# A two-block transformer kernel: the first weight tiles behind a juncture are split by VectorE, later ones wait for the last sums, and the lead's second loads come later

## The chip, the cores and the metric

One NeuronCore of a Trainium2 chip. The metric is the device time of one execution, in microseconds. The engines are called PE (TensorE, matrix products), DVE (VectorE), ACT (ScalarE), POOL (GpSimd) and SP (SyncE, which here only issues DMAs); each works through its own instructions in a fixed order, and semaphores hold an instruction back until what it needs is done.

## The reference

Two depth-2 stacks run one after the other on 512 tokens of width 1024, in fp32: two attention layers (here "block1"), then two layers of FFN, token mixer, FFN. Each branch is normed, projected, and its output is normed again and added to x.

```python
def rms_norm_2(x, gain):
    xf = x.astype(jnp.float32)
    y = xf * lax.rsqrt(jnp.mean(xf * xf, axis=-1, keepdims=True) + NORM_EPS)
    return (y * gain).astype(x.dtype)

def swiglu(h, w_in, w_out):
    gu = h @ w_in
    g, u = jnp.split(gu, 2, axis=-1)
    return (jax.nn.silu(g) * u) @ w_out
...
def second_block(x, norm_gain, ffn_w_in, ffn_w_out, mix_w_in, ...):
    for layer in range(DEPTH):
        g = norm_gain[layer]
        h = swiglu(rms_norm_2(x, g[0]), ffn_w_in[layer, 0], ffn_w_out[layer, 0])
        x = x + 0.5 * rms_norm_2(h, g[1])
        h = token_mixer(rms_norm_2(x, g[2]), mix_w_in[layer], ...)
        x = x + rms_norm_2(h, g[3])
        h = swiglu(rms_norm_2(x, g[4]), ffn_w_in[layer, 1], ffn_w_out[layer, 1])
        x = x + 0.5 * rms_norm_2(h, g[5])
    return x
```

The first stack (`first_block`) is two layers of `x + rms_norm(attention(rms_norm(x) @ w_in) @ w_out)`. The branches in order are block1, block1, ffn0, mixer0, ffn1, ffn2, mixer1, ffn3.

## The kernel before

**Products.** Every fp32 operand is kept as a high and a low part, and each product is three matmuls (`mm3`, L353 high by high, L354 and L355 high by low). x is held transposed, `XT`, as 8 chunks of 128 features by 512 tokens; its high and low parts are `xh` and `xl`.

**Weights.** A weight comes in raws of 128x1024 fp32 (512 KB, tile `wr`, two buffers), loaded by SP (L395). `wsplit` takes a raw in two tiles of 128x512: ACT writes the high part `wh` (L419), then POOL, or DVE where `lo` says so, subtracts it from the raw and writes the low part `wl` (L421). `wh` and `wl` have six buffers each. So a raw's buffer comes free when its second `wl` is written, and PE can use a weight chunk's high part before the low part is there.

**Juncture.** Between two branches stands a `Join`: for both halves of the tokens (t = 0, 1) and four pairs of chunks (i), `front` scales the branch's output and adds it to XT on DVE (L281 or, where a gain of 0.5 is applied, L285; then L287), ACT writes `xh` (L289) and squares (L495), POOL adds the squares up (`sacc`, L498 and L501), and `back` writes `xl` on DVE (L299). `third` does this for t = 1. While this runs, PE already works on the next branch's first two weight units, its "lead" (`lead`): first for t = 0, then for t = 1, one pair of chunks after another as their `xh` and `xl` appear. The row norm itself is applied behind the products, from the sums: a chain of nine small DVE operations (L364 to L372), a transpose that spreads its result (tile `tp`, L438) and an ACT copy (tile `R`, L536). The lead's own weights are loaded and split ahead of the juncture, by `lead_load`, with DVE splits (`lo=nc.vector`, pinned).

**Order.** The kernel is written in program order and a scheduler sets each engine's order when it is built. Two tools bind it: `tc.keep_in_program_order` pins an instruction among the others that are pinned, and `tc.issue_after(x)` holds an instruction behind `x`. `k.gate` uses the second for POOL's weight splits behind a juncture: set at (t, i) == (0, 3), it lets the next eight of them issue only behind the last sum of the first half.

**FFN.** Behind the lead (hidden tiles j = 0 and 1) an FFN takes hidden tiles j = 2, 3, ... over all 512 tokens: per tile two raws (h = 0, 1), 8 chunks, two PSUM banks and 48 matmuls. j = 2 writes to `mm` banks, later ones to `sc`. `act` is on DVE and ACT: `fg` = gate * R (L607), silu (L608), `fu` = up * R (L609), product (L610), high part `ah` on ACT (L611) and low part `al` on DVE (L612). For the lead `act` runs per half: once R of t = 0 is there, and again when R of t = 1 is there. Then four `out_unit`s (p = 0 to 3) multiply by ffn_out, DVE adds the halves (L633). In p = 2 of the second half, `lead_load` loads and splits both parts of the next branch's lead.

The mixer and block1 have the same lead; in block1 the first unit behind it is `tok(0)` (its weights are the stationary operand, 128x256 products), where DVE rotates the results (`ra`, `rb`, L963). In the last unit of `out_proj` (mixer, block1) `lead_load` is called as in the FFN.

Of the kernel before, what the change touches and what calls it, by code (L numbers as in the profile page):

```python
# [210 lines left out]
class Join:  # L211
# [52 lines left out]
    def third(self):  # L264
        self.spread(1)
        self.front(1, 0)
        for i in range(1, 4):
            self.front(1, i)
            self.back(1, i - 1)
        self.back(1, 3)  # L270

    def front(self, t, i):

        k, nc, put = self.k, self.nc, self.put
        v = nc.vector
        sl, c = HALF[t], slice(2 * i, 2 * i + 2)
        if t not in self.scratch:
            self.scratch[t] = (k.mm if t else k.sc)().rearrange("p (a n) -> p a n", a=2)
        s, P = self.scratch[t], self.P[t]
        if self.gpost is None:  # L280
            put(v.tensor_tensor(s, self.Y[:, c, sl], P[:, None, :].to_broadcast([128, 2, 256]), op=OP.mult))  # L281
        else:
            for e in range(2):
                j = 2 * i + e
                put(v.scalar_tensor_tensor(s[:, e], self.Y[:, j, sl], self.gpost[:, j:j + 1], P, op0=OP.mult, op1=OP.mult))  # L285
        x = k.XT[:, c, sl]
        put(v.tensor_tensor(x, x, s, op=OP.add))  # L287
        for j in (2 * i, 2 * i + 1):
            nc.scalar.activation(k.h[0][:, j, sl], k.XT[:, j, sl], AF.Copy, scale=k.gcol(self.nxt[0], j))  # L289
        added = k.square2(k.pre[t], i, x)  # L290
        if (t, i) == (0, 3):
            k.gate = [added, 8]
# [20 lines left out]
class Kern:  # L313
    def __init__(self, ctx, tc, ap):
# [14 lines left out]
        self.gate = None  # L329

# [67 lines left out]
    @contextmanager  # L398
    def behind(self, eng):


        if self.gate and eng is self.nc.gpsimd:
            self.gate[1] -= 1
            with self.tc.issue_after(self.gate[0]):
                yield
            if not self.gate[1]:
                self.gate = None
        else:
            yield

    def wsplit(self, raw, n, lo=None, pool=None, pin=False):
        nc = self.nc
        w = []
        eng = lo or nc.gpsimd
        for c in range(0, n, 2):
# [4 lines left out]
            with self.behind(eng):  # L420
                ins = eng.tensor_tensor(low[:, :m], raw[:, c:c + m], hi[:, :m].bitcast(F32), op=OP.subtract)  # L421
            if pin:
                self.tc.keep_in_program_order(ins)
# [128 lines left out]
    def lead_load(self, nxt, lo=None):  # L552

        if nxt:
            self.lead_w = [[], []]
            for h in range(2):
                for u in range(2):
                    self.lead_w[u] += self.wload(nxt[1][u][h], lo=lo, pool=self.lead_pool, pin=True)
# [35 lines left out]
    def ffn(self, i, gpost, nxt):  # L594
# [19 lines left out]
        def out_unit(half, p):  # L614
            w = []
            for c0 in range(0, FH, 4):
                n = min(4, FH - c0)
                w += self.wload(ap["ffn_out"][i, half, p, :, c0:c0 + n], n)
            last = half == 1 and p == 3
            if half == 1 and p == 2:  # L620
                self.lead_load(nxt, lo=nc.vector)
            for sl in HALF if last else [slice(0, S)]:
                for b in range(2):
                    ps = self.mm()[:, 0:sl.stop - sl.start]
                    for k in range(FH):
                        self.mm3(ps, self.wcol(w[k], slice(b * 128, (b + 1) * 128)), [x[:, sl] for x in acts[k]],
                                 k == 0, k == FH - 1)
                    k = p * 2 + b
# [130 lines left out]
    def out_proj(self, w_ap, OT, gpost, nxt):  # L759
# [7 lines left out]
        with ExitStack() as es:  # L767
            own = Pool(es.enter_context(self.tc.tile_pool(name=f"op{self.leads}", bufs=1, reuse_waits="tile")))
            jobs = [(0, ALL), (1, ALL)] + [(p, h) for h in HALF for p in (2, 3)]
            for p, sl in jobs:  # L770
# [4 lines left out]
                if p == 2 and sl.start == 0:  # L775
                    self.lead_load(nxt, lo=nc.vector)
# [191 lines left out]
    def block1_lead(self, l):  # L968
        return G_PRE + l, (self.ap["w_in"][l, 8], self.ap["w_in"][l, 11])
# [217 lines left out]
    def mixer_lead(self, l):  # L1187
        return G_NORM + l * 6 + 2, (self.ap["mix_in"][l, 6], self.ap["mix_in"][l, 7])

    def ffn_lead(self, l, i):  # L1190
        return G_NORM + l * 6 + 4 * i, (self.ap["ffn_in"][2 * l + i, 0], self.ap["ffn_in"][2 * l + i, 1])
# [308 lines left out]
    def run(self, nl1, nl2):  # L1500
# [15 lines left out]
        self.lead_load(branches[0][2], lo=self.nc.vector)  # L1516
# [96 lines left out]
```

## Time and profile before

| | |
|---|---|
| time, median of 3 runs (lowest to highest) | 2846.74 us (2845.9 to 2852.84) |
| profiled execution: its time, its span | 2845.98 us, 2844.0 us |
| PE busy, share of the span | 2741.8 us, 96% |
| DVE, ACT, POOL busy | 1412.6, 1374.1, 1356.5 us |
| `wl` on POOL (L421) | 732 instructions, mean 1297 ns, 942.0 us |
| `wl` on DVE (L421) | 104 instructions, mean 889 ns |
| PE waited for `xl` (L299) | 16.2 us, 21 times, at most 1.3 us |
| mean granted PE clock | 0.992 of full |

The span is that of the profiled execution; its own time lies 2.0 us over it. In a row of the timeline the first number is the start from the span's begin, the second the duration, both in us; `xcount` is how many like instructions a row stands for (its time is then that from the first's start to the last's end), and the bracket gives the engine's idle time before the row and what ended it. The starts of PE's rows are what to go by: a matmul's shown duration overlaps the next one's.

### The profile page before, as it was taken

Reading aid. Unit: us, or ns where it says so; the run is one execution under the profiler, and the core shown is the slowest. Engines: PE = TensorE matmul, PEld = TensorE weight load, DVE = VectorE, ACT = ScalarE, POOL = GpSimd, SP = SyncE. Lnnn points to the kernel's source line nnn. Section 1 sums busy time; section 2 is a strip of 40 time slices with the busy share of each in tenths; the row PEclk is TensorE's granted clock in tenths of the full one; section 3 lists DMA queues with packets and bytes.
Section 4 is the critical chain, followed back from the end, with each engine's and each line's share of the span. In section 5 each row is a group of like instructions: output and inputs, shape, how many; then the busy total and the mean of one; then the engine's idle time right before and its main releaser. Section 6 shows DMA issues by size and latency. Waiting matters only on the chain.

```text
span 2844.0 us, 42873 instructions
## 1 busy us (share of the span) xinstructions
PE 2741.8 (96%) x16080; PEld 2398.0 (84%) x16080; DVE 1412.6 (50%) x2988; ACT 1374.1 (48%) x2881; POOL 1356.5 (48%) x1327
## 2 busy tenths in 40 slices
PE   8999999999999999899999999999998899999998
PEld 8997899788888887898988888888887798888887
DVE  6589757986302266747630225312336747731132
ACT  5678547874333335657433334333334758433332
POOL 4553365424444455443544445444455543544545
PEclk9999999999999999999999999999999999999999
DMA  5111221112333222121223232233222120223332
GB/s 176 60 46 38 75 72 46 45 66 75 96 92 103 85 81 83 51 79 62 78 96 96 97 93 93 89 89 104 95 77 86 62 81 31 90 82 91 105 99 77
DMA packets 69280, 230.53 MB, mean 81 GB/s; under 512 B 8968, under 2 KB 11912, under 8 KB 68816
## 3 DMA queue, kind: packets, MB, share of 16 engines
q1 hardware_dynamic: 69072, 227.78, 24.5%
q8 instruction: 127, 2.08, 0.3%
q14 instruction: 81, 0.66, 0.1%
HBM read 225.51 MB, written 2.24 MB: 80 GB/s over the span
## 4 chain that ended last, share of the span: by engine, by line
PE 74%; DVE 15%; ACT 4%; issue 3%; POOL 2%; DMA 2%; SPq 0%; POOLq 0%; DVEq 0%; ACTq 0%
PE sc L354 11%; PE sc L353 11%; PE sc L355 11%; PE mm L355 11%; PE mm L353 11%; PE mm L354 11%; DVE xl L299 2%; PE sc L116 2%; PE tp L145 1%; DVE pl L149 1%; DVE XT L287 1%; DVE nm L192 1%; DVE E L204 1%; PE tp L817 1%; POOL wl L421 1%
## 5 line engine op out<-in xcount | busy, mean ns | idle before, releaser
L421 POOL TENSOR_TENSOR wl<-wr,wh 128x512 fp32r<-128x512 f32 x732 | 942.0, 1297 | 883.0 <-ACT wh L419 858.9
L419 ACT CAST wh<-wr 128x512 fp32r<-128x512 f32 x836 | 500.5, 612 | 722.8 <-PE sc L354 450.9
L354 PE MATMUL sc<-xl,wh 128*128 128x512 f32 (+1 forms) x1824 | 658.0, 361 | 16.3 <-DVE xl L299 16.2
L355 PE MATMUL sc<-xh,wl 128*128 128x512 f32 (+1 forms) x1824 | 654.5, 359 | 0.2 <-DVE wl L421 0.2
L353 PE MATMUL sc<-xh,wh 128*128 128x512 f32 (+1 forms) x1824 | 653.2, 360 | 0.0
L607 DVE TENSOR_TENSOR fg<-sc,R 128x512 f32<-128x512 f32 (+1 forms) x92 | 59.3, 644 | 747.6 <-PE sc L355 724.5
L354 PEld LDWEIGHTS sc<-xl,wh 128*128 128x128 f32 x1824 | 344.0, 189 | 72.1 <-DVE xl L299 20.7
L355 PEld LDWEIGHTS sc<-xh,wl 128*128 128x128 f32 x1824 | 344.2, 189 | 51.8 <-DVE wl L421 0.4
L353 PEld LDWEIGHTS sc<-xh,wh 128*128 128x128 f32 x1824 | 342.5, 189 | 51.5
L355 PE MATMUL mm<-ah,wl 128*128 128x512 f32 (+1 forms) x792 | 291.0, 367 | 6.5 <-POOL wl L421 6.5
L353 PE MATMUL mm<-ah,wh 128*128 128x512 f32 (+1 forms) x792 | 290.3, 367 | 1.9 <-ACT wh L419 1.9
L354 PE MATMUL mm<-al,wh 128*128 128x512 f32 (+1 forms) x792 | 289.3, 365 | 0.0
L353 PE MATMUL mm<-wh,xh 128*128 128x256 f32 x960 | 275.0, 286 | 0.0
L354 PE MATMUL mm<-wl,xh 128*128 128x256 f32 x960 | 273.2, 285 | 0.0
L355 PE MATMUL mm<-wh,xl 128*128 128x256 f32 x960 | 273.0, 284 | 0.0
L353 PE MATMUL mm<-xh,wh 128*128 128x512 f32 (+1 forms) x560 | 196.7, 353 | 10.5 <-DVE big L789 3.4
L355 PE MATMUL mm<-xh,wl 128*128 128x512 f32 (+1 forms) x560 | 194.8, 348 | 7.8 <-POOL wl L421 7.8
L354 PE MATMUL mm<-xl,wh 128*128 128x512 f32 (+1 forms) x560 | 193.9, 346 | 0.0
L354 PEld LDWEIGHTS mm<-wl,xh 128*128 128x128 f32 x960 | 184.1, 192 | 1.3
L353 PEld LDWEIGHTS mm<-wh,xh 128*128 128x128 f32 x960 | 183.9, 192 | 1.0
L355 PEld LDWEIGHTS mm<-wh,xl 128*128 128x128 f32 x960 | 184.0, 192 | 0.9
L355 PEld LDWEIGHTS mm<-ah,wl 128*128 128x128 f32 x792 | 149.2, 188 | 33.8 <-POOL wl L421 9.6
(348 smaller groups left out, 4878.1 us busy)
## 6 DMA issues: line engine op xcount, KB each, us to landing
wr<-in_ffn_in_dram SPq DMA_DIRECT2D x176, 512.0 KB, 3.3
wr<-in_ffn_out_dram SPq DMA_DIRECT2D x64, 512.0 KB, 3.6
wr<-in_mix_in_dram SPq DMA_DIRECT2D x56, 512.0 KB, 3.3
wr<-in_w_in_dram SPq DMA_DIRECT2D x48, 512.0 KB, 3.3
wr<-in_ffn_out_dram SPq DMA_DIRECT2D x32, 384.0 KB, 3.1
wr<-in_w_out_dram SPq DMA_DIRECT2D x16, 512.0 KB, 3.3
wr<-in_mix_out_dram SPq DMA_DIRECT2D x16, 512.0 KB, 3.3
Mb<-Md SPq DMA_DIRECT2D x16, 256.0 KB, 3.1
```

The source lines that it names most:

```text
L116: nc.tensor.matmul(sc[:, e], q, kk[:, :n], start=j == 0, stop=j == len(self.K) - 1)
L145: nc.tensor.transpose(p[:, j * per + e], E[i + e][:, j * 128:(j + 1) * 128], self.k.ident)
L149: nc.vector.tensor_tensor(pl[:, :nk, sl], pv, ph[:, :nk, sl].bitcast(F32), op=OP.subtract)
L192: nc.vector.tensor_reduce(nm, sc, axis=AX.X, op=OP.max, negate=True)
L204: nc.vector.scalar_tensor_tensor(E[tb, 0], E[tb, 1], cc[:, i:i + 1], E[tb, 0], op0=OP.mult, op1=OP.add)
L299: self.put(self.nc.vector.scalar_tensor_tensor(lo, k.XT[:, j, sl], k.gcol(self.nxt[0], j), hi.bitcast(F32), op0=OP.mult, op1=OP.subtract))
L353: mm(out, lhs[0], rhs[0], start=start, stop=False, skip_group_check=shared)
L354: mm(out, lhs[0], rhs[1], start=False, stop=False, skip_group_check=shared)
L355: mm(out, lhs[1], rhs[0], start=False, stop=stop, skip_group_check=shared)
L419: nc.scalar.copy(hi[:, :m], raw[:, c:c + m])
L421: ins = eng.tensor_tensor(low[:, :m], raw[:, c:c + m], hi[:, :m].bitcast(F32), op=OP.subtract)
L607: nc.vector.tensor_tensor(g, ps[0], R[:, sl], op=OP.mult)
```

## The change

Three parts:

1. At the start of `third`, `k.ahead` is set to 6 (3 where the next branch is a mixer). The next `ahead` weight tiles that POOL would split go to DVE, pinned in program order. There are seven junctures with a next branch: five with 6 and two with 3, so 36 splits move.
2. The gate is set at (t, i) == (1, 3), for the 8 - `ahead` splits that follow on POOL: these wait for the last sum of the second half.
3. `lead_load` takes h: the lead's first raws come at p = 2, its second ones at p = 3. In the FFN, `out_load(p + 1)` stands at the end of unit p, ahead of its last DVE addition, where the load and its splits stood at the start of unit p + 1.

```diff
     def third(self):
         self.spread(1)
+        self.k.ahead = self.nxt[2]
         self.front(1, 0)
...
-        if (t, i) == (0, 3):
-            k.gate = [added, 8]
+        if (t, i) == (1, 3):
+            k.gate = [added, 8 - k.ahead]
...
-    @contextmanager
-    def behind(self, eng):
-        if self.gate and eng is self.nc.gpsimd:
-            self.gate[1] -= 1
-            with self.tc.issue_after(self.gate[0]):
-                yield
...
     def wsplit(self, raw, n, lo=None, pool=None, pin=False):
...
-        eng = lo or nc.gpsimd
...
             nc.scalar.copy(hi[:, :m], raw[:, c:c + m])
-            with self.behind(eng):
+            eng, held, order = lo or nc.gpsimd, None, pin
+            if eng is nc.gpsimd and self.ahead:
+                self.ahead -= 1
+                eng, order = nc.vector, True
+            elif eng is nc.gpsimd and self.gate:
+                self.gate[1] -= 1
+                held = self.gate[0]
+                if not self.gate[1]:
+                    self.gate = None
+            with self.tc.issue_after(held) if held else nullcontext():
                 ins = eng.tensor_tensor(low[:, :m], raw[:, c:c + m], hi[:, :m].bitcast(F32), op=OP.subtract)
-            if pin:
+            if order:
                 self.tc.keep_in_program_order(ins)
...
-    def lead_load(self, nxt, lo=None):
+    def lead_load(self, nxt, h, lo=None):
         if nxt:
-            self.lead_w = [[], []]
-            for h in range(2):
-                for u in range(2):
-                    self.lead_w[u] += self.wload(nxt[1][u][h], lo=lo, pool=self.lead_pool, pin=True)
+            if h == 0:
+                self.lead_w = [[], []]
+            for u in range(2):
+                self.lead_w[u] += self.wload(nxt[1][u][h], lo=lo, pool=self.lead_pool, pin=True)
...
         def out_unit(half, p):
-            w = []
+            if not ahead:
+                out_load(half, p)
+            w = ahead[:]
+            ahead.clear()
             last = half == 1 and p == 3
-            if half == 1 and p == 2:
-                self.lead_load(nxt, lo=nc.vector)
+            if half == 1 and p >= 2:
+                self.lead_load(nxt, p - 2, lo=nc.vector)
...
+                    if b and p < 3:
+                        out_load(half, p + 1)
```

The built programs show where the scheduler put the moved splits. In each row below, the first number is the place on its engine, then come line, operation and tiles (numbers behind a name tell buffers and raws apart), and what the instruction waits for. DVE, at the start of ffn1's work behind its lead: before, the last `al` of the first half is followed by the second half's rms chain.

```order
1831 L612 TENSOR_TENSOR al_16504<-fu_16506,ah_16503 128x256 [waits Activation_49]
1832 L612 TENSOR_TENSOR al_16514<-fu_16516,ah_16513 128x256 [waits Activation_49]
1833 L364 TENSOR_SCALAR rnx_16557<-tp_16554 128x2 [waits PE_49]
...
1851 L612 TENSOR_TENSOR al_16514<-fu_16621,ah_16513 128x256 [waits Activation_49]
1852 L610 TENSOR_TENSOR fu_16637<-fu_16637,fg_16636 128x512 [waits DVE_49]
1853 L612 TENSOR_TENSOR al_16635<-fu_16637,ah_16634 128x512 [waits Activation_49]
1854 L607 TENSOR_TENSOR fg_16716<-sc_16644,R_16118 128x512 [waits PE_49]
```

The same place on DVE of the changed kernel:

```order
1846 L611 TENSOR_TENSOR al_16504<-fu_16506,ah_16503 128x256 [waits Activation_49]
1847 L611 TENSOR_TENSOR al_16514<-fu_16516,ah_16513 128x256 [waits Activation_49]
1848 L420 TENSOR_TENSOR wl_16535<-wr_16532,wh_16534 128x512 [waits DMAHW5_49]
1849 L420 TENSOR_TENSOR wl_16539<-wr_16532,wh_16538 128x512
1850 L366 TENSOR_SCALAR rnx_16557<-tp_16554 128x2 [waits PE_49]
...
1871 L609 TENSOR_TENSOR fu_16637<-fu_16637,fg_16636 128x512 [waits DVE_49]
1872 L611 TENSOR_TENSOR al_16635<-fu_16637,ah_16634 128x512 [waits Activation_49]
1873 L420 TENSOR_TENSOR wl_16649<-wr_16646,wh_16648 128x512 [waits DMAHW1_49]
1874 L420 TENSOR_TENSOR wl_16653<-wr_16646,wh_16652 128x512
1875 L606 TENSOR_TENSOR fg_16716<-sc_16644,R_16118 128x512 [waits PE_49]
```

The splits of j = 2 (`wl_16535`, `wl_16539`) now stand behind the last `al` of the first half, and those of j = 3 (`wl_16649`, `wl_16653`) behind j = 2's own `al_16635`. On POOL of before, these four stand at rows 662, 663, 669 and 670, between the sums of the two halves.

PE of before, where j = 2 starts (`mm_16530`, `mm_16531`):

```order
8055 L353 MATMUL mm_16530<-xh_84,wh_16534 128x512 [waits PE_49]
8056 L354 MATMUL mm_16530<-xl_85,wh_16534 128x512
8057 L355 MATMUL mm_16530<-xh_84,wl_16535 128x512 [waits Pool_49]
8058 L353 MATMUL mm_16531<-xh_84,wh_16534 128x512
8059 L354 MATMUL mm_16531<-xl_85,wh_16534 128x512
```

PE of the changed kernel, at the start of j = 2 and of j = 3 (`sc_16644`, `sc_16645`):

```order
8055 L355 MATMUL mm_16530<-xh_84,wh_16534 128x512 [waits PE_49]
8056 L356 MATMUL mm_16530<-xl_85,wh_16534 128x512
8057 L355 MATMUL mm_16531<-xh_84,wh_16534 128x512
8058 L356 MATMUL mm_16531<-xl_85,wh_16534 128x512
8059 L472 MATMUL tp_16554<-ones_94,sacc_16308 128x1 [waits PE_49,Pool_49]
8060 L472 MATMUL tp_16554<-ones_94,sacc_16308 128x1
8061 L357 MATMUL mm_16530<-xh_84,wl_16535 128x512 [waits DVE_49]
...
8107 L355 MATMUL sc_16644<-xh_84,wh_16648 128x512 [waits Activation_49]
8108 L356 MATMUL sc_16644<-xl_85,wh_16648 128x512
8109 L355 MATMUL sc_16645<-xh_84,wh_16648 128x512
8110 L356 MATMUL sc_16645<-xl_85,wh_16648 128x512
8111 L357 MATMUL sc_16644<-xh_84,wl_16649 128x512 [waits DVE_49]
```

The four products that need only the high part are pulled together ahead of the first that needs the low part, and that one waits for DVE now. Third place, ACT of before in the last `out_unit`s of ffn0, where `wr_11619` and `wr_11629` are the lead's second raws and `wr_11721` is ffn_out's first raw of p = 3:

```order
1053 L419 CAST wh_11631<-wr_11629 128x512 [waits DMAHW7_49]
1054 L419 CAST wh_11635<-wr_11629 128x512
1055 L485 ACTIVATE sq_11674<-big_9312 128x256 [waits DVE_49,Pool_49]
1056 L485 ACTIVATE sq_11677<-big_9312 128x256 [waits Pool_49]
1057 L419 CAST wh_11723<-wr_11721 128x512 [waits DMAHW4_49,PE_49]
```

The same rows of the changed kernel, where the lead's second raws are called `wr_11731` and `wr_11741` and ffn_out's is `wr_11694`:

```order
1053 L407 CAST wh_11743<-wr_11741 128x512 [waits DMAHW7_49]
1054 L407 CAST wh_11747<-wr_11741 128x512
1055 L484 ACTIVATE sq_11654<-big_9312 128x256 [waits DVE_49,Pool_49]
1056 L484 ACTIVATE sq_11657<-big_9312 128x256 [waits Pool_49]
1057 L407 CAST wh_11696<-wr_11694 128x512 [waits DMAHW4_49,PE_49]
```

The names have changed, and the places by content have not: the lead's casts stand ahead of those of p = 3 in both.

## Rows read from the trace of the kernel before

**Rows 1.** The page: the span, and each engine's busy time.

```profile
span 2844.0 us, 42873 instructions
...
PE 2741.8 (96%) x16080; PEld 2398.0 (84%) x16080; DVE 1412.6 (50%) x2988; ACT 1374.1 (48%) x2881; POOL 1356.5 (48%) x1327
```

**Rows 2.** Timeline of the juncture ahead of ffn1, second half: POOL, DVE, PE.

```profile
1388.89 2.70 POOL L421 TENSOR_TENSOR wl<-wr,wh 128x512 fp32r<-128x512 f32 x2
...
1389.22 2.65 DVE L299 SCALAR_TENSOR_TENSOR xl<-XT,gains,xh 128x256 fp32r<-128x256 f32 x2
...
1390.50 0.38 PE L354 MATMUL sc<-xl,wh 128*128 128x256 f32 x1 [1.21 <-DVE xl L299]
...
1397.22 0.39 PE L354 MATMUL sc<-xl,wh 128*128 128x256 f32 x1 [0.43 <-DVE xl L299]
```

**Rows 3.** Line L299 by itself: durations ns, smallest, median, largest.

```profile
L299 DVE SCALAR_TENSOR_TENSOR xl<-XT,gains,xh x112: 467/950/1510, 346.0 to 2486.2; 128x256 fp32r<-128x256 f32 x112
```

**Rows 4.** Timeline of the juncture ahead of mixer0, second half: PE.

```profile
1048.87 0.39 PE L354 MATMUL sc<-xl,wh 128*128 128x256 f32 x1 [1.34 <-DVE xl L299]
...
1052.80 0.39 PE L354 MATMUL sc<-xl,wh 128*128 128x256 f32 x1 [0.81 <-DVE xl L299]
```

**Rows 5.** Timeline of ffn1 behind its lead: PE's j = 2, DVE's and ACT's `act`.

```profile
1403.16 0.40 PE L353 MATMUL mm<-xh,wh 128*128 128x512 f32 x1
...
1404.79 0.76 DVE L610 TENSOR_TENSOR fu<-fu,fg 128x256 f32<-128x256 f32 x2 [0.31 <-ACT fg L608]
...
1405.25 0.41 ACT L611 CAST ah<-fu 128x256 fp32r<-128x256 f32 x1 [0.18 <-DVE fu L610]
...
1405.68 0.43 DVE L612 TENSOR_TENSOR al<-fu,ah 128x256 fp32r<-128x256 f32 x1
...
1405.90 0.50 PE L473 MATMUL tp<-ones,sacc 128*128 128x1 f32 x4
...
1406.26 0.49 PE L353 MATMUL mm<-xh,wh 128*128 128x512 f32 x1
```

**Rows 6.** Timeline of DVE in ffn0's last units: two splits back to back.

```profile
1007.52 1.29 DVE L421 TENSOR_TENSOR wl<-wr,wh 128x512 fp32r<-128x512 f32 x2 [5.04 <-ACT wh L419]
```

**Rows 7.** Timeline of ffn1: the second half's `act`, and PE's start of j = 3.

```profile
1414.03 0.42 DVE L607 TENSOR_TENSOR fg<-sc,R 128x256 f32<-128x256 f32 x1 [4.25 <-ACT R L536]
...
1414.80 0.39 PE L353 MATMUL sc<-xh,wh 128*128 128x512 f32 x1
...
1419.63 1.01 DVE L612 TENSOR_TENSOR al<-fu,ah 128x512 fp32r<-128x512 f32 x1 [0.69 <-ACT ah L611]
```

**Rows 8.** Windows (start:end length; engines' busy us; PEclk third from the end).

```profile
1170.00:1172.30 2.30, 0.01 (x1) 0.01 (x1) 0.75 (x2) 1.75 (x6) 2.16 (x3) 1.00 0.00 0
...
1173.10:1179.60 6.50, 6.29 (x25) 5.74 (x25) 5.44 (x19) 2.31 (x10) 2.66 (x4) 0.50 0.35 121
...
1110.77:1114.90 4.13, 4.13 (x10) 3.27 (x11) 0.00 (x0) 0.00 (x0) 3.66 (x3) 0.50 0.39 126
...
1762.30:1766.00 3.70, 3.08 (x23) 2.82 (x23) 3.63 (x5) 2.29 (x6) 3.54 (x5) 1.00 0.65 237
```

**Rows 9.** Waits of PE by releaser: us in total, times, longest us.

```profile
PE mm L355 <- POOL wl L421: 14.4, 17, 3.9
```

**Rows 10.** Timeline of the second block1 behind its lead: PE's first product, DVE.

```profile
377.62 0.28 PE L353 MATMUL mm<-wh,xh 128*128 128x256 f32 x1
...
380.25 0.14 DVE L1015 TENSOR_SCALAR subg<-subg 128x1 f32<-128x1 f32 x1
...
390.04 0.42 DVE L963 TENSOR_TENSOR ra<-mm,lin 128x256 f32<-128x256 f32 x1 [3.50 <-POOL wl L421]
```

**Rows 11.** Timeline of mixer0 behind its lead: DVE, PE's first product.

```profile
1062.20 1.29 DVE L1201 TENSOR_TENSOR O<-sc,R 128x512 f32<-128x512 f32 x2 [1.74 <-ACT R L536]
...
1062.30 0.40 PE L353 MATMUL mm<-xh,wh 128*128 128x512 f32 x1
```

**Rows 12.** Timeline of ACT in ffn0's last units: the lead's second raw.

```profile
1006.87 1.14 ACT L419 CAST wh<-wr 128x512 fp32r<-128x512 f32 x2 [6.59 <-DMA wr<-in_mix_in_dram]
```

More of the change, by code (lines that the diff above doesn't have):

```diff
@@ L1 @@
 import math
-from contextlib import ExitStack, contextmanager
+from contextlib import ExitStack, nullcontext
 import numpy as np
@@ L329, in __init__ @@
         self.gate = None
+        self.ahead = 0
     def tp(self):
@@ L396, in wload @@
         return self.wsplit(raw, n, lo, pool, pin)
-    @contextmanager
-    def behind(self, eng):
-        if self.gate and eng is self.nc.gpsimd:
-            self.gate[1] -= 1
-            with self.tc.issue_after(self.gate[0]):
-                yield
[L406 to L409, printed above, removed]
     def wsplit(self, raw, n, lo=None, pool=None, pin=False):
@@ L612, in act, with out_load, out_unit @@
             nc.vector.tensor_tensor(al, u, ah.bitcast(F32), op=OP.subtract)
-        def out_unit(half, p):
-            w = []
+        ahead = []
+        def out_load(half, p):
             for c0 in range(0, FH, 4):
                 n = min(4, FH - c0)
-                w += self.wload(ap["ffn_out"][i, half, p, :, c0:c0 + n], n)
+                ahead.extend(self.wload(ap["ffn_out"][i, half, p, :, c0:c0 + n], n))
+        def out_unit(half, p):
+            if not ahead:
+                out_load(half, p)
+            w = ahead[:]
+            ahead.clear()
             last = half == 1 and p == 3
-            if half == 1 and p == 2:
-                self.lead_load(nxt, lo=nc.vector)
+            if half == 1 and p >= 2:
+                self.lead_load(nxt, p - 2, lo=nc.vector)
             for sl in HALF if last else [slice(0, S)]:
@@ L774, in out_proj @@
                     ws[p] += self.wload(w_ap[p][1], pool=pool, raws=self.wp)
-                if p == 2 and sl.start == 0:
-                    self.lead_load(nxt, lo=nc.vector)
+                if p >= 2 and sl.start == 0:
+                    self.lead_load(nxt, p - 2, lo=nc.vector)
                 for b in range(2):
@@ L968, in block1_lead @@
     def block1_lead(self, l):
-        return G_PRE + l, (self.ap["w_in"][l, 8], self.ap["w_in"][l, 11])
+        return G_PRE + l, (self.ap["w_in"][l, 8], self.ap["w_in"][l, 11]), 6
     def block1(self, l, nxt):
@@ L1187, in mixer_lead @@
     def mixer_lead(self, l):
-        return G_NORM + l * 6 + 2, (self.ap["mix_in"][l, 6], self.ap["mix_in"][l, 7])
+        return G_NORM + l * 6 + 2, (self.ap["mix_in"][l, 6], self.ap["mix_in"][l, 7]), 3
     def ffn_lead(self, l, i):
-        return G_NORM + l * 6 + 4 * i, (self.ap["ffn_in"][2 * l + i, 0], self.ap["ffn_in"][2 * l + i, 1])
+        return G_NORM + l * 6 + 4 * i, (self.ap["ffn_in"][2 * l + i, 0], self.ap["ffn_in"][2 * l + i, 1]), 6
     def mixer(self, l, nxt):
@@ L1515, in run @@
             self.load_x()
-        self.lead_load(branches[0][2], lo=self.nc.vector)
+        for h in range(2):
+            self.lead_load(branches[0][2], h, lo=self.nc.vector)
         self.prenorm(branches[0][2][0])
```

## The prediction

> **What bounds the kernel now.** I read the page first. PE is busy 2741.8 us of a span of 2844.0 [rows 1], so about 102 us of its idle time is all there is to win, and whatever makes PE wait is lost at once. I then went through PE's waits in the timeline and looked at what stands ahead of each. At the junctures it is `xl`. With POOL's splits running beside it (1388.89, 2.70 us for two), two `xl` take 2.65 us, and PE waits 1.21 and later 0.43 us [rows 2]. Alone an `xl` takes as little as 0.467 us [rows 3], so each takes 1.3 where it could take half a microsecond. At the junctures with the 0.5 gain PE waits 1.34 and 0.81 us [rows 4]. That is the stall the change goes at. Then I read the stretch just behind the juncture, where PE does not wait at all today: that is where the moved splits now stand, so I took every duration there.
>
> **What the removal of POOL's splits from the second half gives.** With no split beside it, the first `xl` of 1389.22 ends at about 1389.69 in place of 1390.44, so the wait of 1.21 shrinks to 0.47; the wait of 0.43 goes. That is 1.17 us per juncture [rows 2, 3]. There are four of this form (ahead of the second block1, ffn0, ffn1, ffn3). At the other three (ahead of mixer0, ffn2, mixer1) the first wait falls by 0.82 (the first `xl` there took 1.30) and the second by its 0.81, so 1.63 [rows 3, 4]. Together 4 x 1.17 + 3 x 1.63 = 9.6 us. From below: nothing, if POOL's running sums, which stay, slow `xl` by themselves (its median is 0.950 [rows 3]).
>
> **What the moved splits cost at an FFN's start.** DVE works in order. The splits of j = 2 now stand behind the first half's `act`, those of j = 3 behind j = 2's. Before, both were done on POOL before PE came there.
>
> First wait. PE starts j = 2 at 1403.16; 12 products until 1405.90 give 0.23 us each [rows 5]. In the changed order it can do four products (0.91) and the ones-products (1406.26 less 1405.90, 0.36) and wants the first low part at 1404.43. DVE ends the second `fu` at 1405.55, ACT the second `ah` 0.41 after the first, at 1406.07, and `al` takes 0.43, so the split starts at 1406.50 [rows 5]. A split takes 0.65 on DVE where POOL is quiet [rows 6], and the low part is there at about 1407.2. **PE waits 2.8 us.**
>
> Second wait. Counted from the second half's R, which moves along with PE: DVE starts its `act` at 1414.03 and j = 2's own `al` at 1419.63, PE starts j = 3 at 1414.80 [rows 7]. PE wants j = 3's low part four products later, at 1415.7. That `al` took 1.01 beside a POOL split; alone I take 0.7 (the split of the same size, rows 6), so the split starts at 1420.3 and ends at 1421.0. **PE waits 5.3 us** (5.6 with 1.01). The raws behind these two splits come free later too, but the next ones are wanted a full hidden tile (48 products, 11 us) later; a load, a cast and a POOL split have to fit in that, and I count nothing there. All four FFNs start with this order.
>
> **What the waits do to PE's clock.** After PE had been idle from 1170.00 to 1172.30, its granted clock was 0.50, the 1.2 GHz level, from 1173.10 for 6.5 us; after the wait that ended at 1110.77 it was 0.50 until 1114.90, 4.13 us [rows 8]. That wait is the longest one for a POOL split, 3.9 us [rows 9]. After the wait of 1.33 that ended at 1762.30 it stayed 1.00 [rows 8]. At half clock half of the time is lost. For the first wait (2.8) the nearest row is the one of 2.30: at most 3.2 us lost, and less if the low level begins within the wait, so 2.6. For the second (5.3) the nearest is that of 3.9: 2.1. Both lie between 0 (no fall) and 3.2.
>
> The Trainium skill (TensorE: Matmul & The Clock Gate, HAM oscillation — how this bites in real kernels) says that PE drops to its lower clock after long idle gaps between bursts and pays for each again, and the trace agrees for the gap of 3.9. By that rule gaps below its limit cost nothing, the first wait might be one of them, and the sum would be some 13 us lower; the fall after 2.30 us speaks against it. This is one of the rivals below, worked out there from rows.
>
> So an FFN's start costs 2.8 + 5.3 + 2.6 + 2.1 = 12.8, four of them 51.2, and with their gains (3 x 1.17 + 1.63 = 5.1) **+46.1 us**.
>
> **The second block1.** Its four first splits stand on DVE behind `subg`, which ends at 380.39; PE, from 377.62, wants the first at 378.2 (two products at half of 0.23, as they are half as wide, and the ones-products), and has it at 381.1 [rows 6, 10]. Wait 2.9, clock 2.6. The next two splits stand behind the four rotations of the unit's second half, about 1.4 to 1.7 (0.42 each, overlapping), and PE wants them at once: 1.4 + 0.7 - 0.2 = 1.9 [rows 6, 10]. A wait of 1.9 lies between the 1.33 that left the clock alone and the 2.30 that did not; I take no fall. Less 1.17: **+6.2**.
>
> **The mixers.** Only three splits move. They stand behind two `O` (to 1063.49); the low part is there at 1064.15 and wanted at 1062.30 + 0.92 + 0.36 = 1063.6, a wait of 0.55 [rows 5, 6, 11]. The third split stands inside the second rms chain and may hold PE as long again, up to 0.85; I take 1.0 for both. No clock. Less 1.63: **-0.6 each, -1.3** for two.
>
> **The lead's second loads.** In the last `out_unit`s ACT waits 6.59 us for the lead's second raw, and the casts of p = 3 stand behind it [rows 12]. The code moves the call, but the built order of ACT and SP is the same by content as before, so this wait stays: 0. DVE's splits of that raw now stand behind the additions of p = 2 and run beside POOL's splits of p = 3; that may add up to 0.4 per FFN, and nothing waits for the splits themselves before the juncture. At `out_proj` the order is unchanged as well.
>
> **Sum.** 46.1 + 6.2 - 1.3 = +51.0. On the profiled execution's 2845.98 that is 2897.0. The median of the three runs is 2846.74, 0.8 above it, which I leave aside: **2897 us**.
>
> **The rivals.**
> - *The first, shorter waits leave the clock alone*: without 4 x 2.6 and block1's 2.6 the sum is 51.0 - 13.0 = 38.0, 2884 us. For it: no row shows a gap of just 2.8. Against it: 2.30 was enough at 1172.30 [rows 8]. This is the case of the Trainium skill's rule named above.
> - *No fall at all*: another 4 x 2.1 less, +29.6, 2876 us. Against it: the row of 1110.77 [rows 8].
> - *The sums slow `xl` as the splits did*, and the gain of 9.6 is not there: +60.6, 2907 us. For it: the median of 0.950 [rows 3]. Against it: PE waits longest just where a split lies beside `xl` [rows 2].
> - *The later loads do free p = 3*: the casts there stop waiting [rows 12], and I bound the gain by 3 us in each of three FFNs: 2888 us. Against it: the built order.
> - *The other side: DVE has time.* If the moved splits are done before PE wants them, only the gains are left: 2845.98 - 9.6 = 2836 us. The place is DVE between 1403 and 1406.5: this decides as soon as the two waits of an FFN's start together fall below 1.2 us, in place of 8.1. The pieces of `act` ahead of the splits would have to take almost no time [rows 5, 7].
> - *A draw*: waits so short, with no clock, that they cancel the gains, 2846 us.
>
> **How the numbers follow.** Forecast 0.52, first waits without clock 0.18, no clock 0.08, no gain at `xl` 0.09, p = 3 freed 0.05, DVE in time 0.05, a draw 0.03. This kernel's time can be told from no change at about 0.3%, 8.5 us. Faster by more: 0.05; within: 0.03; slower: 0.92. The bounds: with no clock 2876, less 2 for the reading of the durations, is 2874; with 3.2 us for each of the FFNs' eight waits and for both of block1's (the second had none) in place of what I took, 4 x (0.6 + 1.1) + 0.6 + 3.2 = 10.6 more, 2908, and 3 for the longer `al` (0.3 x 4) and the splits of p = 3 gives 2911. The range 2874 to 2911 leaves out the two cases at 2836 and 2846 and the tails.
>
> **What would show it.** In the changed profile: PE waits for DVE's `wl` (L420) of 2 to 3 us at each FFN's start and of about 5 us at its j = 3, some 40 us in all; a granted clock of 0.50 behind them; `xl` below its mean of before, and the waits for it down from 1.2 to 0.5; the ACT wait of 6.6 us ahead of p = 3 unchanged. If PE's waits for DVE's `wl` are short, the prediction is wrong at its first step, and if they are long and the clock stays at 1.00, at its third.

## The result, and the profile after

The changed kernel takes 2890.61 us (median of four; 2886.42 to 2894.36) and the kernel before 2848.49 (four runs): ratio 1.0146, interval 1.0133 to 1.0158. It is slower by 42 us by the medians. The two profiled executions, 2894.36 (the slowest of its four) and 2845.98 us, lie 48.4 apart, and it is this difference that the rows below explain. The prediction was 2897, its range 2874 to 2911. All ratios are of fast executions alone, while the medians 2850.38 and 2852.18 below include one slow execution each (3811 and 3017 us).

The page of the changed kernel, against [rows 1]: the span grew by 47.9 us, PE's busy time by 15.7 of them.

```profile
span 2891.9 us, 42851 instructions
...
PE 2757.5 (95%) x16080; PEld 2409.4 (83%) x16080; DVE 1421.9 (49%) x3024; ACT 1373.8 (48%) x2881; POOL 1306.5 (45%) x1291
```

PE's waits by releaser (us in total, times, longest). Two lines are new, 29.6 us for splits on DVE, nearly all of it at the FFNs' starts (the second block1's 2.6 us stand in a third). The waits for `xl`, 16.2 us before, are down to 6.5.

```profile
PE sc L357 <- DVE wl L420: 19.2, 5, 4.7
...
PE mm L357 <- DVE wl L420: 10.4, 6, 2.5
...
PE sc L356 <- DVE xl L300: 6.5, 11, 0.9
```

The timeline of the changed kernel where ffn1 starts, PE, DVE and ACT in order of time, answers to [rows 5] and [rows 7]. PE does four products of j = 2 and the ones-products and then waits. DVE has the first half's `act` ahead of the two splits: its `fu` waits for the silu of ACT, which itself waits for R (1420.64) and loads a table for 1.28 us; `al` and the splits follow without a gap, and the first split ends just before PE goes on. At j = 3 the same happens behind j = 2's own `act`.

```profile
1420.64 0.37 ACT L535 COPY R<-tp 128x256 f32<-128x256 f32 x1 [4.14 <-PE tp L437]
1421.03 1.28 ACT L607 ACT_TABLE_LOAD   x1
1421.15 0.40 PE L355 MATMUL mm<-xh,wh 128*128 128x512 f32 x1
...
1422.77 0.76 DVE L609 TENSOR_TENSOR fu<-fu,fg 128x256 f32<-128x256 f32 x2 [0.31 <-ACT fg L607]
1423.67 0.76 DVE L611 TENSOR_TENSOR al<-fu,ah 128x256 fp32r<-128x256 f32 x2
1424.35 1.29 DVE L420 TENSOR_TENSOR wl<-wr,wh 128x512 fp32r<-128x512 f32 x2
1425.09 0.73 PE L357 MATMUL mm<-xh,wl 128*128 128x512 f32 x2 [2.51 <-DVE wl L420]
...
1435.42 0.39 PE L355 MATMUL sc<-xh,wh 128*128 128x512 f32 x1
...
1439.89 0.69 DVE L611 TENSOR_TENSOR al<-fu,ah 128x512 fp32r<-128x512 f32 x1 [0.69 <-ACT ah L610]
1440.50 1.28 DVE L420 TENSOR_TENSOR wl<-wr,wh 128x512 fp32r<-128x512 f32 x2
1441.24 1.22 PE L357 MATMUL sc<-xh,wl 128*128 128x512 f32 x2 [4.75 <-DVE wl L420]
```

Windows of the changed kernel just behind such waits (PEclk is the third figure from the end): ffn1's first wait, ffn1's second, ffn3's first, ffn0's first, ffn0's second, ffn2's first. Only the first window, behind a wait of 2.51 us, has the full clock. Behind the other waits PE ran at the 1.2 GHz level, also where the wait was as long (ffn3, 2.51) or shorter (ffn2, 2.31).

```profile
1425.20:1428.50 3.30, 3.30 (x15) 2.73 (x16) 3.01 (x12) 0.00 (x0) 0.00 (x0) 1.00 0.49 159
1441.30:1446.80 5.50, 5.50 (x13) 4.33 (x14) 0.48 (x1) 1.47 (x3) 1.06 (x1) 0.50 0.52 194
...
2533.00:2536.00 3.00, 3.00 (x8) 2.31 (x8) 1.71 (x6) 0.79 (x2) 0.00 (x0) 0.50 0.64 190
...
697.10:700.50 3.40, 3.40 (x8) 2.75 (x9) 3.05 (x12) 0.00 (x0) 0.00 (x0) 0.50 0.49 154
...
716.10:720.00 3.90, 3.90 (x9) 3.05 (x10) 0.46 (x1) 0.06 (x1) 0.00 (x0) 0.50 0.61 209
...
1805.80:1808.80 3.00, 3.00 (x8) 2.35 (x9) 2.72 (x12) 0.00 (x0) 0.00 (x0) 0.50 0.53 176
```

**Where the 48 us went.** I compared the start of the same PE product in both traces. At ffn1, j = 2 starts at 1403.16 before and at 1421.15 after, 17.99 later; j = 3 at 1414.80 and 1435.42, 20.62 later. So the first wait cost 2.6. By the middle of j = 3 (1422.96 and 1451.43) the lag is 28.5: the second cost 7.9. Over the four FFNs:

| | ffn0 | ffn1 | ffn2 | ffn3 | sum | PE's idle time in it |
|---|---|---|---|---|---|---|
| first wait | 5.5 | 2.6 | 4.0 | 4.3 | 16.4 | 9.8 |
| second wait | 7.0 | 7.9 | 7.9 | 6.7 | 29.4 | 19.0 |

So the FFN starts cost 45.8 us, of which 28.8 are idle time; 17.0 are not. The second block1 lost 7.9 us behind its lead, and ffn0's p = 3 lost 2.8. At the seven junctures PE came 13.0 us earlier in all (1.5 to 2.3 each); the mixers and smaller places lost 4.4 of that again.

### The profile page after: what moved, and what is told of

Read it like the earlier page. It is cut to its first block, busy times and chain, and to the rows that moved or that the text cites. A ratio compares the mean times of both kernels' runs of the same rounds, so it can differ in the third digit from the quotient of the medians.

```text
span 2891.9 us, 42851 instructions
## 1 busy us (share of the span) xinstructions
PE 2757.5 (95%) x16080; PEld 2409.4 (83%) x16080; DVE 1421.9 (49%) x3024; ACT 1373.8 (48%) x2881; POOL 1306.5 (45%) x1291
## 4 chain that ended last, share of the span: by engine, by line
PE 73%; DVE 15%; ACT 5%; issue 3%; POOL 2%; DMA 1%; SPq 0%; POOLq 0%; DVEq 0%; ACTq 0%
PE sc L357 11%; PE sc L356 11%; PE sc L355 11%; PE mm L357 11%; PE mm L355 10%; PE mm L356 10%; PE sc L116 2%; PE tp L145 1%; DVE pl L149 1%; POOL wl L420 1%; DVE xl L300 1%; DVE nm L192 1%; DVE wl L420 1%; DVE E L204 1%; PE tp L825 1%
## 5 line engine op out<-in xcount | busy, mean ns | idle before, releaser
L420 POOL TENSOR_TENSOR wl<-wr,wh 128x512 fp32r<-128x512 f32 (+1 forms) x696 | 893.4, 1293 | 935.1 <-ACT wh L407 888.0
L357 PE MATMUL mm<-ah,wl 128*128 128x512 f32 (+1 forms) x792 | 291.8, 368 | 10.4 <-POOL wl L420 10.3
L357 PE MATMUL mm<-xh,wl 128*128 128x512 f32 (+1 forms) x560 | 197.2, 354 | 18.2 <-DVE wl L420 10.4
```

The costliest lines, as they stand in the source:

```text
L357: mm(out, lhs[1], rhs[0], start=False, stop=stop, skip_group_check=shared)
```

## The experiments

**Each part alone.** First the gate alone: in the kernel before, `(t, i) == (0, 3)` becomes `(1, 3)`, and all eight splits stay on POOL.

> The kernel before with the gate's place alone changed: set at (1, 3) with a count of 8, all splits stay on POOL. If the loss comes from where the splits stand on DVE, nothing of it is here: the waits for xl fall from 16.2 to about 6.5 us as in the changed kernel, POOL starts j = 2's splits behind the last sum and has the first done before PE wants it, no wait for a wl of more than 0.5 us at an FFN's start, and the time is 10 to 13 us under before (ratio 0.9955 to 0.9965). If holding POOL's splits back is itself what costs (late low parts, raws freed late), the waits for wl show here on POOL and the time is 10 us or more above before.

Measured: 2863.15 us against 2850.55, ratio 1.0043 (1.0030 to 1.0056). Neither theory had this. The waits for `xl` did fall, and no low part was late, but a new wait took their place:

```profile
PE tp L438 <- DVE r L372: 17.7, 7, 2.9
...
PE sc L354 <- DVE xl L299: 6.4, 11, 0.9
```

Its timeline at the juncture ahead of ffn1 (POOL, DVE, PE) shows why. POOL starts its four splits as soon as the last sum is done, just when DVE runs the first half's rms chain. The chain's operations on 128x2 take 0.16 us when POOL is quiet; here four in a row take 1.2 each, and each ends within 0.1 us of a POOL split's end.

```profile
1405.23 4.99 POOL L421 TENSOR_TENSOR wl<-wr,wh 128x512 fp32r<-128x512 f32 x4
1405.33 1.21 DVE L366 TENSOR_TENSOR rnt<-r 128x2 f32<-128x2 f32 x1
1406.57 1.22 DVE L367 SCALAR_TENSOR_TENSOR rnt<-rnt,rnx 128x2 f32<-128x2 f32 x1
1407.82 1.20 DVE L368 SCALAR_TENSOR_TENSOR r<-rnt,r 128x2 f32<-128x2 f32 x1
1409.05 1.18 DVE L369 TENSOR_TENSOR rnt<-r 128x2 f32<-128x2 f32 x1
1410.27 0.16 DVE L370 TENSOR_TENSOR rnt<-rnt,rnx 128x2 f32<-128x2 f32 x1
...
1410.97 0.41 PE L438 MATMUL tp<-ident,r 128*128 128x128 f32 x2 [2.54 <-DVE r L372]
```

So the later hold moves the collision from `xl` to the chain. In the changed kernel at ffn1 POOL has no split to run there, since the moved ones are on DVE, and PE has no wait for the chain's `r` at any juncture.

Then the moved splits alone, with the gate set at (0, 3) and the loads as before, and the third part alone (gate and splits as before).

> The first part alone: 36 splits go to DVE, pinned; the gate is set at (0, 3) as before (with 8 less the splits moved), and the lead's loads come as before. If DVE's order is the cause, the waits of 2.5 and 4.7 us at each FFN's start are all here, and the time is 43 to 48 us above before (ratio 1.015 to 1.017), a little less than the whole change by what p = 3 costs there. If the gate or the loads carry a good part of the loss, it is under +30 us.

> The third part alone: the lead's second raws at p = 3 and out_load at the unit's end; no split moves and the gate is as before. By the built order the casts stand where they stood, so the wait of ACT of 6.6 us stays; DVE's four splits of these raws run beside POOL's of p = 3 and each slows the other (1.72 in place of 1.28 us on POOL in the changed kernel), so 0 to 4 us above before (ratio 1.000 to 1.0015). If the later loads freed p = 3, it is 5 to 9 us under before; if they are a main part of the loss, 10 us or more above.

Measured: 2888.97 us, ratio 1.0134 (1.0120 to 1.0147), 38 us above the kernel before (43 to 48 expected), with the same two waits (19.0 and 10.4 us) and the same 6.5 us for `xl`; and 2850.38 us, ratio 0.9994 (0.9985 to 1.0004). So the loss is that of the moved splits, and the gain at `xl` is theirs too. The gate's later place costs something by itself (above), but beside the moved splits nothing of it can be measured: 1.0134 without it and without the later loads, 1.0146 with both, and the intervals overlap. The third part does nothing that can be measured either.

**Four splits in place of six** at block1 and the FFNs:

```diff
-        return G_NORM + l * 6 + 4 * i, (...), 6
+        return G_NORM + l * 6 + 4 * i, (...), 4
```

> The whole change with 4 in place of 6 splits moved (mixers still 3): the splits of j = 3 stay on POOL, behind the last sums. If each wait has its own price, the second waits (4.7 us, and the 1.2 GHz stretch behind each) are gone and the first stay: 4 x (4.7 + 1.9) + 1.6 for the second block1, so 28 us under the changed kernel, some 17 to 20 above before (ratio 1.006 to 1.007). If the second wait only takes over what the first leaves (the same lateness passed on), the time is within 10 us of the changed kernel.

Measured: 2858.48 us, ratio 1.0028 (1.0017 to 1.0039), 32 us under the changed kernel (28 expected). PE's second waits are gone, since j = 3's splits are on POOL again; the first stay, as the waits of this run show:

```profile
PE mm L357 <- DVE wl L420: 10.4, 6, 2.5
```

The second waits cost 29.4 by the table above; that and block1's second wait (2.0 idle) make up the 32. The ratio lies under the 1.006 to 1.007 expected, which took these 28 off the 48 us of the profiled pair; by the medians the loss is 42.

**What the clock takes.** PE gets matmuls to do in place of waiting; their result is thrown away:

```diff
                         w = self.wload(ap["ffn_in"][i, half * FH + j, h])
+                        if half == 0 and h == 0 and j < 4:
+                            for _ in range(10 if j == 2 else 20):
+                                nc.tensor.matmul(ps[0], w[0][0][:, 0:128], xh[:, 0], start=True, stop=True)
```

> The changed kernel, with PE given matmuls whose result is thrown away at the start of hidden tiles j = 2 (10 of 128x512) and j = 3 (20) of each FFN: 2.3 and 4.6 us at 0.23 each, that is about as long as PE idled there (2.5 and 4.75 us). Theory (beyond the idle time itself, what the FFN starts cost is PE's clock falling to 0.50 behind the wait): the granted clock stays 1.00 behind the filled waits, each FFN's start costs some 7.5 us in place of 11.4, and the time is 13 to 18 us under the changed kernel's, ratio 1.008 to 1.010 to the kernel before. Rival (the rest of the loss is something else, such as later splits and raws that come late in a chain behind the waits): the time stays the changed kernel's, ratio 1.0145, or more with the added work.

Measured: 2876.23 us, ratio 1.0093 (1.0078 to 1.0109), 14.4 us under the changed kernel with 120 matmuls more. The window over ffn1's start of this run has the full clock from end to end, and what PE still waited there is short:

```profile
1415.80:1445.00 29.20, 27.63 (x124) 22.54 (x123) 13.53 (x35) 10.14 (x20) 6.06 (x5) 1.00 0.20 72
```

```profile
1419.54 0.73 PE L357 MATMUL mm<-xh,wl 128*128 128x512 f32 x2 [0.25 <-DVE wl L420]
...
1429.88 4.70 PE L664 MATMUL sc<-xh,wh 128*128 128x512 f32 x20
...
1436.80 0.73 PE L357 MATMUL sc<-xh,wl 128*128 128x512 f32 x2 [1.32 <-DVE wl L420]
```

Counted as in the table above, the four FFN starts cost 31.7 us in this run in place of 45.8: 27.2 for the added matmuls, 2.8 that PE still waited and 1.7 more. So most of the 17.0 us that were not idle time were the clock.

**The place or the engine?** First the moved splits without the pin, so that the scheduler places them:

```diff
-                eng, order = nc.vector, True
+                eng = nc.vector
```

> The changed kernel with the moved splits on DVE but not pinned: the scheduler then puts all six far ahead, among the first half's additions and xl of the juncture. Theory (the pinned place is what costs): no wait for DVE's wl at the FFN starts, and the time is at or a little over that of before, ratio 0.998 to 1.005, with the rest from the splits (0.65 us each) that stand ahead of the first half's xl. Rival (36 more splits on DVE cost of themselves): over 1.010.

Measured: 2852.22 us, ratio 1.0013 (1.0004 to 1.0022): the same 36 splits on DVE, 38 us less than pinned. The waits for late low parts at the FFN starts are gone. At ffn1 the waits for the second half's `xl` are as short as in the changed kernel (under 0.5), but each juncture has a new one of 1.0 to 1.6 us: a moved split now stands ahead of the first half's first `xl`, so that the waits for `xl` come to 14.6 us in all. The two mixers also wait 1.5 us each for `r`. DVE and PE of this run at the juncture ahead of ffn1:

```profile
1376.38 0.69 DVE L420 TENSOR_TENSOR wl<-wr,wh 128x512 fp32r<-128x512 f32 x1
...
1378.32 1.10 DVE L300 SCALAR_TENSOR_TENSOR xl<-XT,gains,xh 128x256 fp32r<-128x256 f32 x2
...
1379.08 0.39 PE L356 MATMUL sc<-xl,wh 128*128 128x256 f32 x1 [1.03 <-DVE xl L300]
```

Second, four splits, those of the FFNs written directly behind the first half's chain, ahead of the `act`. A callback that `lead` runs behind `pre_cols(0)` does it:

```diff
+        def cols():
+            self.pre_cols(0)
+            if early:
+                early()
...
-        self.after(12, lambda: self.pre_cols(0))
+        self.after(12, cols)
...
+   early=lambda: two.extend(self.wload(ap["ffn_in"][i, 2, h]) for h in range(2))
```

> The changed kernel with four splits moved at FFNs and block1 (three at mixers), and in the FFNs these four (of j = 2) written, and pinned, directly behind the first half's rms chain, ahead of the first half's act. DVE had nothing to do there for 2.5 us (it waits for R), and four splits take 2.6 to 2.7. Theory (the cost comes from the place of the splits on DVE, not from DVE doing them): the first waits of the four FFN starts (10.4 us) and the clock behind them vanish, and the time is some 14 to 18 us under that of the run with four splits (2858), so 2840 to 2844, ratio 0.996 to 0.998. Rival (splits ahead of the act delay the act and with it PE's banks or the second half): PE waits 1 us or more per FFN for act's banks, ratio 1.000 to 1.003.

Measured: 2852.18 us, ratio 1.0006 (0.9997 to 1.0015). The FFNs' first waits are gone, which settles that the place was the cost; but the rival was right that the gain at `xl` does not come through. PE waits for r again, at the second half's transposes:

```profile
PE tp L437 <- DVE r L374: 4.5, 4, 1.6
```

**Attempts to keep the gain.** Four more versions look for a place where the splits harm nothing. In the first the hold of the kernel before is set behind the last operation of the first half's chain:

> The kernel before, with POOL's eight splits held behind the last operation of the first half's rms chain in place of the last sum of the first half; nothing is moved to DVE. Theory (what the hold shifts about is only which DVE work a POOL split runs beside; with the sums' hold it was the nine small operations of the chain, so a hold behind that chain costs nothing): PE's waits for xl fall from 16.2 to about 6.5 us, PE's waits of 2.5 us at the seven transposes behind the chain stay away, the first low parts are there about 1.4 us behind the chain's end, before PE wants them, and the time is 9 to 13 us under that of before, ratio 0.9955 to 0.997. Rival (the splits then run beside the first half's act and the second half's chain and are late or slow those down): PE waits 1 to 3 us per juncture behind the lead, ratio 1.000 to 1.004.

Measured: 2854.18 us, ratio 1.0019 (1.0010 to 1.0029). The edit did not do what I had written: the hold names an operation of DVE, and POOL's splits were not held behind it. What ran is the kernel before without a hold. At mixer0 its splits ran among the first half's sums (1036.53, 1039.74 and 1040.97), ahead of the chain that they were to follow, and PE waited 2.07 us at 1046.06 for `rny`, the norm of the branch's own output in the second half. So the hold of the kernel before is itself worth some 5 us.

To make POOL really wait, a copy of 128x2 on POOL reads r, and the hold is set behind that:

```diff
     def pre_cols(self, t):
         self.rms(self.pre[t], self.r[:, 2 * t:2 * t + 2])
+        if t == 0 and self.joined:
+            self.gate = [self.nc.gpsimd.tensor_copy(self.pre[t]["acc"][:, 0:2], self.r[:, 0:2]).ins, 8]
```

> The kernel before, with the eight splits on POOL held behind a copy of 128x2 on POOL that reads the first half's r, so that POOL really waits there for the end of the first half's rms chain (the hold behind an instruction of DVE had bound nothing on POOL). Nothing is moved to DVE. Theory (a POOL split costs PE time only where it lies beside DVE work that PE waits for: xl, and the nine small operations of the chain): PE's waits for xl fall from 16.2 to about 6.5 us, there is no wait for r at the transposes of the first half, the first low part is there some 1.6 us behind the chain's end where PE wants it about 4 us behind it, and the time is 6 to 12 us under that of before, ratio 0.996 to 0.998. Rival (the splits now run beside the first half's act and the second half's chain, which slow down in turn and hold PE's transposes of the second half): PE waits 1 us or more per juncture for r or for wl, ratio 1.000 to 1.003.

Measured: 2870.82 us, ratio 1.0080 (1.0067 to 1.0093). The chain is quick and the first low part in time, yet PE waits 15.7 us for r, five times (the longest, 4.7 at the second block1, I did not trace back); at ffn1 it is the r of the second half, 3.16 us at 1421.93. The timeline of ACT at ffn1 shows a route that neither theory had. A raw's buffer comes free with its second split; the splits are later, so the next raw is later, and its cast stands ahead of the silu in ACT's order. ACT idles 3.61 us for the raw, then loads the table; before, the table was loaded at once behind R, at 1403.04.

```profile
1408.06 0.37 ACT L538 COPY R<-tp 128x256 f32<-128x256 f32 x1 [4.14 <-PE tp L438]
1412.04 0.62 ACT L419 CAST wh<-wr 128x512 fp32r<-128x512 f32 x1 [3.61 <-DMA wr<-in_ffn_in_dram]
1412.68 1.28 ACT L610 ACT_TABLE_LOAD   x1
```

The `act`, and with it the second half's chain behind it on DVE, is late by that.

Next, only j = 2's first two splits early, of four:

> As the run with four early splits, but only j = 2's first two stand directly behind the first half's rms chain; its other two stand behind the second half's chain, as the scheduler places them. Theory (four splits of 0.68 fill more than the 2.5 us that DVE had free, so the act, and with it the second half's chain, was late by 1 to 1.6 us and PE waited 4.5 us in all at the transposes of the second half; two splits fit): these waits go, and the time is 3 to 6 us under that of the run with four early ones (2852), ratio 0.9975 to 0.9995 to the kernel before. Rival (the other two splits are late in turn, since the second half's chain stands ahead of them): PE waits for DVE's wl about 1 us per FFN, ratio 1.000 to 1.002.

Measured: 2854.85 us, ratio 1.0029 (1.0018 to 1.0039). The rival holds: the other two stand behind the second half's chain and are late, by 2.0 to 2.5 us per FFN and not 1, with 9.6 us of waits for `wl` in all:

```profile
PE mm L357 <- DVE wl L420: 9.6, 6, 2.5
```

Last, three early at the FFNs, block1 and the mixers left as before:

> Splits are moved at the four FFN junctures only, three each (j = 2's first three), written and pinned directly behind the first half's rms chain; the five that follow there wait on POOL for the last sums, the first of them beside that chain. At block1 and the mixers the hold and the splits are those of the kernel before. Theory (the FFN gains at xl, 3 x 1.17 + 1.63 = 5.1 us, are had without a late low part: three splits take 2.0 us of the 2.5 that DVE had free, and one POOL split beside the chain delays r by about 1.1, less than it can be late without holding PE): the time is 2 to 6 us under that of before, ratio 0.998 to 0.9993. Rival (any delay of the chain or of the act there returns in the second half's chain, as in the run with four, 4.5 us): ratio 0.9995 to 1.002.

Measured: 2858.06 us, ratio 1.0030 (1.0020 to 1.0039). PE waits 10.3 us for r, and ACT's rows at ffn1 show the same route as above, 3.03 us for the raw ahead of the silu:

```profile
1406.91 0.37 ACT L535 COPY R<-tp 128x256 f32<-128x256 f32 x1 [4.14 <-PE tp L437]
1410.32 0.62 ACT L407 CAST wh<-wr 128x512 fp32r<-128x512 f32 x1 [3.03 <-DMA wr<-in_ffn_in_dram]
1410.95 1.28 ACT L613 ACT_TABLE_LOAD   x1
```

The run with four early splits has this route too. What I had taken for the cause there, that four splits are more than DVE had time for, its rows at ffn1 contradict: the four take 2.49 us, DVE starts `fg` 0.15 us after it has gone idle, as soon as R is there, and what comes late is the silu, behind a cast that waits 1.86 us for its raw.

```profile
1400.69 2.49 DVE L420 TENSOR_TENSOR wl<-wr,wh 128x512 fp32r<-128x512 f32 x4
...
1403.34 0.43 DVE L612 TENSOR_TENSOR fg<-sc,R 128x256 f32<-128x256 f32 x1 [0.15 <-ACT R L535]
...
1405.17 0.62 ACT L407 CAST wh<-wr 128x512 fp32r<-128x512 f32 x1 [1.86 <-DMA wr<-in_ffn_in_dram]
```

No version was measured faster than the kernel before. Whether a third buffer for raws, or silu ahead of that cast in ACT's order, would keep the gain was not tried.

## Why the prediction was right, point by point

- **The gain at `xl`: right in the waits, too small in time.** Forecast 9.6 us; PE's waits for `xl` went from 16.2 to 6.5, 9.7 less, but the starts of PE's products show 13.0 us gained at the junctures, so more than the waits alone. The sums do slow `xl` too, but little: one line of the changed kernel by itself (ns: smallest, median, largest) has half the median of [rows 3], and some `xl` that still take a microsecond. That rival (2907) fell.

```profile
L300 DVE SCALAR_TENSOR_TENSOR xl<-XT,gains,xh x112: 467/480/1022, 344.9 to 2521.9; 128x256 fp32r<-128x256 f32 x112
```

- **First wait, forecast 2.8: 2.31 to 2.51.** The four products, the ones-products and the split behind `fu`, `ah` and `al` came as worked out. PE goes on 3.94 us behind j = 2's start (1421.15 to 1425.09), forecast 4.04; the rest is that the ones-products end 0.15 later than I had put them, so that less of the time counts as idle.
- **Second wait, forecast 5.3: 4.74 and 4.75.** The splits do follow j = 2's `al`, which took 0.69 (estimated 0.7); but the whole `act` was quicker with POOL quiet: from its first `fg` to that `al` it took 5.24 us (1434.65 to 1439.89) in place of 5.60 [rows 7]. The wait was 0.4 shorter by that, and a little by the end of the four products.
- **The clock, forecast 2.6 and 2.1 behind each: right in kind, the first mis-sized.** 7 of 8 waits were followed by the 1.2 GHz level (the second ones of ffn2 and ffn3, not shown above, by a granted clock of 0.50 over 1824.00 to 1828.50 and 0.59 over 2549.30 to 2553.50). Beyond idle time the first waits cost 6.6 in all (forecast 10.4) and the second 10.4 (forecast 8.4). Filling the waits took 14.4 of these 17.0 away, so the step is shown, not argued. The Trainium skill (TensorE: Matmul & The Clock Gate, HAM oscillation — how this bites in real kernels) says that PE pays for each long gap again. The second waits agree with this; but the rival made of it, that gaps below its limit cost nothing, agrees with one of the four first waits (ffn1, 2.51, full clock) and not with the other three of the same length or less. Which first wait is followed by the low level is not settled by its place or its length: in the run of the moved splits alone it was ffn1's (2.52) and not ffn3's (2.51), as the windows behind these two show. What decides it no run here tells.

```profile
1420.70:1424.00 3.30, 3.30 (x9) 2.61 (x10) 3.02 (x12) 0.00 (x0) 0.00 (x0) 0.54 0.46 158
...
2524.60:2528.00 3.40, 3.34 (x15) 2.76 (x16) 3.12 (x13) 0.00 (x0) 0.00 (x0) 1.00 0.47 154
```

- **Block1, forecast +6.2: about +6.4, in part by luck.** The first wait cost 4.0 in all where 5.5 was forecast: 2.17 us idle in place of 2.9, and less for the clock (0.65 over 378.10 to 383.00). The second place cost 4.0 in place of 1.9: beside 1.60 and 0.39 us, PE waited 0.57 and 0.26 for POOL's next splits (396.08 and 397.32), which I had not counted; the clock stayed at 1.00 there, as forecast. The juncture ahead gave 1.6 in place of 1.17.

```profile
377.98 0.39 PE L356 MATMUL mm<-wl,xh 128*128 128x256 f32 x1 [2.17 <-DVE wl L420]
392.92 0.35 PE L355 MATMUL mm<-wh,xh 128*128 128x256 f32 x1 [1.60 <-DVE rb L971]
393.66 0.39 PE L356 MATMUL mm<-wl,xh 128*128 128x256 f32 x1 [0.39 <-DVE wl L420]
```

- **The mixers, forecast -0.6 each: nothing gained.** The first wait was 0.28 where 1.0 had been taken for both, but what the juncture gained was lost again some 50 us later: there PE waits 3.10 us for ACT's `wh`, where it waited 1.44 before (1106.12). PE came earlier, the cast did not: ahead of mixer0's juncture the changed kernel is 18.9 us behind the other, and at this product 19.0; in mixer1 it is 38.1 and 38.0. I had not looked that far.

```profile
1125.12 0.50 PE L355 MATMUL mm<-xh,wh 128*128 128x512 f32 x1 [3.10 <-ACT wh L407]
```

- **The third part, forecast 0: right.** ACT still waits for the lead's second raw, 7.02 us against the 6.59 of [rows 12]. Its side effect, forecast at up to 0.4 per FFN, was 2.8 in ffn0 of the profiled run: there POOL's and DVE's splits ran beside each other and took 1.6 us each, four on either engine,

```profile
1029.18 6.32 POOL L420 TENSOR_TENSOR wl<-wr,wh 128x512 fp32r<-128x512 f32 x4
1029.42 6.63 DVE L420 TENSOR_TENSOR wl<-wr,wh 128x512 fp32r<-128x512 f32 x4
```

  and the clock fell for 3 us behind (1037.80 to 1040.80, 0.50). The other FFNs lost little there, and alone this part measured as nothing. Nor is the whole 2.8 shown to be its effect: in its own profile ffn0's p = 3 lost 0.6, and in that of the moved splits alone, where the loads are as before, 0.5.

The sum of forecast terms was +51.0, the profiled pair gave +48.4 and the medians +42.1. The terms missed by more than the sum did: the FFN starts cost 45.8 in place of 51.2 and the junctures gave 13.0 in place of 9.6, while p = 3, the mixers and smaller places cost some 5 us more than forecast. That these misses nearly balance is luck; the waits, their places and the fall of the clock behind most of them came as reasoned. The difference between the last two is between executions of the same kernels and is not assigned to any step.

## What to carry to other kernels

A split that is moved to another engine costs what stands ahead of it there: the same 36 splits cost 42 us pinned behind `act` and 4 where the scheduler put them. Before a piece of work is delayed to relieve a neighbour, list what its end releases, buffers and loads included; here every later place for the splits met a chain that PE waits for, by DVE's small operations or by a raw that came late ahead of a silu. And an idle stretch of 2.3 us on PE can cost nearly twice its length (ffn2: 4.0), where the clock falls behind it.

## What was not expected of the hardware

- Beside back-to-back splits of 1.25 us on POOL, DVE operations on 128x2 that take 0.16 us alone took 1.18 to 1.22, each ending within 0.1 us of a split, while 128x512 splits on both engines (p = 3 above) both went to about 1.6 us from 1.29 and 0.65: in these rows the small operations lose far more, in proportion. Not every DVE operation is slowed: in the kernel before, the addition of L287, one operand of which lies in a PSUM bank (`mm`), took 0.69 us at 1387.16 beside POOL's splits (1386.20, 5.39 us for four), and the same addition in the changed kernel (L288, 1406.71) took 0.69 with POOL quiet.
- The same idle time of 2.51 us was followed by the 1.2 GHz level at ffn0 and ffn3 and by the full clock at ffn1, in one execution; in the run of the moved splits alone, 2.52 at ffn0 and ffn1 was followed by the low level and 2.51 at ffn3 by the full clock.
